# A two-layer hybrid block on one core: the instruction order from the tile scheduler's timeline simulation

## The chip, the cores and the metric

The program runs on one core of a Trainium2 chip. The time is the device time of one execution in microseconds (us). A core has a matrix engine (PE), a vector engine (DVE), a scalar engine (ACT), GpSimd (POOL) and a queue that issues transfers (SP). Each engine takes its instructions strictly in the order of its own program, and semaphores make it wait for the others. The change is about that order and about nothing else.

## What is computed

Two layers of a block for 256 tokens of `x` and 256 of a context, width 1024, all in float32. Each layer normalises, mixes tokens by three branches (a spatial gate, a differential attention, a gated delta net in both directions), merges them, and ends in a gated convolution network of width 2816. Cut to what matters:

```python
for l in range(DEPTH):                                   # DEPTH = 2
    mod_x, mod_c = silu(c) @ w_mod[l] + b_mod[l], silu(c_ctx) @ w_mod[l] + b_mod[l]
    h_x = modulate(rms_norm(x, norm1_g[l]), sh1_x, sc1_x)     # and h_c for the context
    (u, sv, bq, bk, bv, dq, dk, dv, dz, beta, a, gate) = split_in(h @ w_in[l])
    ya = gelu(u) * (w_s @ rms_norm(gelu(sv)) + b_s)           # spatial gating
    p = softmax(q k^T); yb = rms_norm((p[:, 0] - lam * p[:, 1]) @ v)   # differential attention
    # gated delta net, chunks of 64 tokens, both directions
    u, w = triangular_solve(I + A, v * beta), triangular_solve(I + A, k * beta * exp(G))
    def step(state, blk):
        v_new = u_c - w_c @ state
        o_c = qd_c @ state + intra_c @ v_new
        state = state * g_tot + k_tail^T @ v_new
    yc = rms_norm(o) * silu(z)
    y = (sig(g0) * (ya @ w_a) + sig(g1) * (yb @ w_b) + sig(g2) * (yc @ w_c)) @ w_o
    x = x + gt1 * y
    x = x + gt2 * (silu(conv(h @ w_up)_gate) * conv(h @ w_up)_val) @ w_down
```

The context is carried through layer 0 only.

## The kernel before

All large products run on PE in three passes of a reduced-precision type: each operand is split into a high and a low part (`wh`, `wl` for weights, `hh`, `hl` for activations), and `wh*hh`, `wl*hh` and `wh*hl` are added up in one PSUM bank. A weight block arrives by SP in `wr` (3 buffers); ACT makes `wh` from it and DVE `wl` (4 buffers each). PSUM has eight banks in four groups: `p` two, `g` three, `a` two and `b` one. Nearly every instruction is recorded at a helper's line (L240 matmul, L237 activation, L219 tensor-tensor, L234 scalar-tensor-tensor, L231 tensor-scalar), so the tile names tell them apart.

The names that the steps below use, in the order of a layer (`mixer`, L629):

- The modulation products `pmod`, `pmc` and `modv` (head of the program), and, for later use, rows of `wmt` with DVE products `mj` (L483), issued ahead of their need.
- `norm_halves` (L539): `pss` and `pb` on PE, `xn` on DVE, then `hh` on ACT and `hl` on DVE, for eight blocks of the width.
- `pu`, `ptm`, `pj`, `pg`: projections by PE, long runs of matmuls that need nothing but weights and `hh`, `hl`. They fill PE while a chain elsewhere goes on. `pj` writes a buffer that the scan's `U` occupies until the scan is done, so `pj` can't start before it.
- `gdn_solve` (L1210): a chain of 31 steps on DVE (`sT`, `sL`) ends in `sLC`; then PE does 128 small products `pZ`, ACT copies them to `sZ` and lays out `U`, PE does 128 products `pU2`, ACT copies those into `U`, DVE scales `U`.
- `gdn_intra` (L1088): `pkv`, `pgram` on PE, `vtok` on ACT, `inT` on DVE.
- `gdn_scan` (L1181) calls `gdn_step` (L1285) eight times. A step can't begin before the state `gS` of the one before it is there, and alternates between PE and DVE:

```python
pk = kT @ S                     # PE, pkS
rhs = pk * neG + vtok           # DVE, four instructions
V = U @ rhs                     # PE, pV
vn = V * tail (and V * r2)      # DVE
pq = qT @ S; po = inT @ vn      # PE, pq and pgo, in the steps that give an output
S = S * gts + ktok^T @ vn       # PE, pS (two products), then DVE, gS
```

- `attn_core` (L871): scores `psc` (PE), maximum `mx` (DVE), exponentials (ACT), `pr` (DVE), transposes `paT` (PE, L907) and their copy `aT` (ACT), `po` (PE), a norm on DVE, transposes `poT` (PE, L922).
- `gdn_out` (L1357): four groups of transposes `pgT` (L1362) in layer 0, two in layer 1, all in the one bank of group `b`; four DVE instructions empty it each time.
- `branch` (L689): `pg` and `pbr`, the latter from the branch's result (`ych`, `ycl` for the delta net).

What sets the order: the kernel's text is one long program, and the scheduler that wraps it (`tile.TileContext`) sorts all instructions of all engines by a simulated machine, which takes from the instructions that are ready. `gdn_keys`, `gdn_solve`, `gdn_intra`, `gdn_scan` and `gdn_out` stand in `tc.high_priority(offset=AHEAD)` blocks, which lets the scheduler put them ahead of work that the text names earlier. Which model of the machine it simulates decides how many matmuls of `pu`, `ptm` or `pg` it puts between two links of a chain.

## Time and profile before

| | |
|---|---|
| median of three runs (lowest, highest) | 1647.09 us (1644.26, 1651.51) |
| the profiled execution | 1642.39 us, its span 1640.6 us |
| PE busy | 1583.4 us, 97% of the span |
| DVE busy | 1207.0 us, 74% |
| ACT busy | 767.9 us, 47% |
| mean granted clock of PE | 0.985 of full speed |

The span runs from the first instruction to the last; 1.8 us of the execution lie outside it. "Busy" is the union of an engine's instructions, so on PE it counts a matmul from its start to its modelled end.

### The profile page before, as it was taken

How to read it: one execution, taken by the hardware profiler on the slowest of the kernel's cores; microseconds unless marked ns; L12 is line 12 of the kernel's file. 1: busy time of each engine (PE TensorE's matmuls, PEld its weight loads, DVE VectorE, ACT ScalarE, POOL GpSimd, SP SyncE). 2: the span in 40 equal slices, each digit the busy share in tenths (PEclk: the TensorE clock that was granted, in tenths of full speed). 3: DMA queues.
4: the chain of work that ended last, by engine and by line, in shares of the span. 5: the costliest groups of instructions: out<-in, count | busy, mean ns of one | idle time of the engine just before them, and what ended most of it. 6: DMA issues, size and time to landing. Idle time of an engine off the chain costs nothing.

```text
span 1640.6 us, 27599 instructions
## 1 busy us (share of the span) xinstructions
PE 1583.4 (97%) x10664; PEld 1346.9 (82%) x10664; DVE 1207.0 (74%) x2831; ACT 767.9 (47%) x1455; POOL 6.6 (0%) x16
## 2 busy tenths in 40 slices
PE   5999999999999998999999999999999999989999
PEld 3777977876788887888888887888878799989998
DVE  5649977788764457999778876659777776788685
ACT  3654461156532333544234443654723754556563
POOL 0000000000000000000000000000000000000000
PEclk9999989999999998999999999999999999989999
DMA  8313321142343433454566565221222246545655
GB/s 340 132 60 110 107 66 53 65 125 69 100 145 94 150 93 101 128 171 160 166 203 201 191 195 182 78 92 53 70 64 83 86 144 223 186 132 180 191 181 154
DMA packets 65283, 218.22 MB, mean 133 GB/s; under 512 B 7552, under 2 KB 13696, under 8 KB 63232
## 3 DMA queue, kind: packets, MB, share of 16 engines
q1 hardware_dynamic: 63280, 208.70, 39.9%
q10 hardware_dynamic: 1872, 7.77, 1.3%
q8 instruction: 83, 1.36, 0.3%
q14 instruction: 48, 0.39, 0.1%
HBM read 213.29 MB, written 3.15 MB: 132 GB/s over the span
## 4 chain that ended last, share of the span: by engine, by line
PE 83%; DVE 7%; ACT 4%; DMA 2%; issue 2%; ACTq 0%; DVEq 0%
PE pup L240 21%; PE pg L240 12%; PE pdn L240 10%; PE pqkv L240 7%; PE pbr L240 6%; PE ptm L240 4%; PE pwo L240 4%; PE pu L240 2%; PE psc L240 2%; PE pj L240 2%; PE pS L240 2%; ACT U L237 1%; DMA wmt<-in_wmt_dram 1%; PE pkS L240 1%; PE po L240 1%
## 5 line engine op out<-in xcount | busy, mean ns | idle before, releaser
L237 ACT ACTIVATE wh<-wr 128x512 fp32r<-128x512 f32 (+1 forms) x594 | 366.7, 622 | 432.1 <-PE pdn L240 91.1
L219 DVE TENSOR_TENSOR wl<-wr,wh 128x512 fp32r<-128x512 f32 (+1 forms) x592 | 399.4, 680 | 156.8 <-ACT wh L237 154.1
L240 PE MATMUL pup<-hh,wh 128*128 128x256 f32 (+1 forms) x720 | 242.3, 337 | 2.2 <-ACT hh L237 2.1
L240 PE MATMUL pup<-hh,wl 128*128 128x256 f32 (+1 forms) x720 | 241.4, 336 | 0.0
L240 PE MATMUL pup<-hl,wh 128*128 128x256 f32 (+1 forms) x720 | 240.3, 335 | 0.0
L240 PEld LDWEIGHTS pup<-hh,wh 128*128 128x128 f32 x720 | 139.1, 193 | 16.8 <-ACT hh L237 2.9
L240 PEld LDWEIGHTS pup<-hh,wl 128*128 128x128 f32 x720 | 139.1, 193 | 13.0
L240 PEld LDWEIGHTS pup<-hl,wh 128*128 128x128 f32 x720 | 138.4, 193 | 13.1
L240 PE MATMUL pg<-hh,wh 128*128 128x512 f32 (+1 forms) x384 | 131.0, 341 | 0.1
L240 PE MATMUL pg<-hh,wl 128*128 128x512 f32 (+1 forms) x384 | 130.4, 339 | 0.2 <-DVE wl L219 0.2
L240 PE MATMUL pg<-hl,wh 128*128 128x512 f32 (+1 forms) x384 | 130.2, 339 | 0.0
L240 PE MATMUL ptm<-wh,hl 128*128 128x256 f32 x448 | 130.2, 291 | 0.0
L240 PE MATMUL ptm<-wl,hh 128*128 128x256 f32 x448 | 129.6, 289 | 0.3 <-DVE wl L219 0.3
L240 PE MATMUL ptm<-wh,hh 128*128 128x256 f32 x448 | 129.4, 289 | 0.0
L234 DVE SCALAR_TENSOR_TENSOR fcv<-pup,par,fcv 128x510 f32<-128x510 f32 (+1 forms) x176 | 107.3, 612 | 26.2 <-ACT fcv L237 26.1
L240 PE MATMUL pdn<-fh,wh 128*128 128x256 f32 (+1 forms) x366 | 121.0, 330 | 0.7 <-ACT fh L237 0.7
L240 PE MATMUL pdn<-fl,wh 128*128 128x256 f32 (+1 forms) x366 | 120.6, 330 | 0.7 <-DVE fl L219 0.7
L240 PE MATMUL pdn<-fh,wl 128*128 128x256 f32 (+1 forms) x366 | 120.7, 330 | 0.0
L483 DVE SCALAR_TENSOR_TENSOR wmt<-wmt,scb 128x1024 f32<-128x1024 f32 x80 | 97.7, 1221 | 23.1 <-DMA wmt<-in_wmt_dram 22.6
L240 PEld LDWEIGHTS ptm<-wh,hh 128*128 128x128 f32 x448 | 86.6, 193 | 2.7 <-issue 2.0
L240 PEld LDWEIGHTS ptm<-wl,hh 128*128 128x128 f32 x448 | 86.6, 193 | 2.5 <-issue 1.7
L240 PEld LDWEIGHTS ptm<-wh,hl 128*128 128x128 f32 x448 | 86.7, 194 | 2.1 <-issue 1.7
(332 smaller groups left out, 3223.1 us busy)
## 6 DMA issues: line engine op xcount, KB each, us to landing
wmt<-in_wmt_dram SPq DMA_DIRECT2D x80, 512.0 KB, 3.6
wr<-in_wup_dram SPq DMA_DIRECT2D x80, 512.0 KB, 3.9
wr<-in_wfm_dram SPq DMA_DIRECT2D x78, 512.0 KB, 3.5
wr<-in_wtm_dram SPq DMA_DIRECT2D x32, 512.0 KB, 3.6
wr<-in_wdn_dram SPq DMA_DIRECT2D x32, 512.0 KB, 3.9
wr<-in_wbr_dram SPq DMA_DIRECT2D x24, 512.0 KB, 3.6
wm<-in_wmod_dram SPq DMA_DIRECT2D x8, 1024.0 KB, 11.0
wr<-in_wo_dram SPq DMA_DIRECT2D x16, 512.0 KB, 3.5
```

Source lines behind the costliest of these rows:

```text
L219: self.nc.vector.tensor_tensor(out=out, in0=a, in1=b, op=op)
L234: self.nc.vector.scalar_tensor_tensor(out=out, in0=a, scalar=s, in1=b, op0=op0, op1=op1)
L237: self.nc.scalar.activation(out, a, f, bias=bias, scale=scale, **k)
L240: self.nc.tensor.matmul(out, lhsT, rhs, start=start, stop=stop, **k)
L483: nc.vector.scalar_tensor_tensor(out=o, in0=w, scalar=1.0, in1=sb[:, v], op0=ALU.mult, op1=ALU.mult, accum_out=m4[:, n % 4, v:v + 1])
```

## The change

One argument is added where the scheduler is created. With it the scheduler simulates the machine by its timeline simulation in place of its default model. No instruction, tile, buffer or transfer is added or taken away by the kernel's text.

```diff
--- before.py
+++ after.py
@@ -1452,7 +1452,7 @@
     out = nc.dram_tensor("out_0_dram", (128, 8, SEQ), F32, kind="ExternalOutput").ap()
-    with tile.TileContext(nc) as tc:
+    with tile.TileContext(nc, schedule_with_timeline_sim=True) as tc:
         body(tc, aps, out)
```

Both programs have the same 9364 matmuls on PE and 2703 instructions on DVE; ACT has the same activations and 25 loads of its function table where there were 29. What differs is the order: nearly all of PE's rows and most of DVE's have moved. Three places follow, all on PE; in a row the tile written stands left of the arrow, with the number that the kernel's text gives it, and `x8` counts equal matmuls in a row.

Place 1, PE between the solve and the scan of layer 0, the last rows ahead of the scan's first `pV`. Before:

```order
L240 MATMUL pgram_2424<-qT_616,kT_188 64x64 x8
L240 MATMUL pu_3056<-hl_125,wh_3063 128x512
L1096 MATMUL pkv_2434<-cst0_77,vT_617 128x128 x4
L240 MATMUL pu_3056<-hh_124,wh_3063 128x512
L240 MATMUL pgram_2440<-qT_616,kT_188 64x64 x8
L240 MATMUL pu_3056<-hh_124,wl_3064 128x512
L1096 MATMUL pkv_2450<-cst0_77,vT_617 128x128 x4
L240 MATMUL pu_3056<-hl_125,wh_3063 128x512
L240 MATMUL pgram_2456<-qT_616,kT_188 64x64 x8
L240 MATMUL pu_3056<-hh_124,wh_3063 128x512
L240 MATMUL pu_3056<-hh_124,wl_3064 128x512
L240 MATMUL pV_2467<-vtok_2401,U_1312 64x128 x8
```

Now:

```order
L1096 MATMUL pkv_2402<-cst0_77,vT_617 128x128 x4
L240 MATMUL psc_3807<-akT_1414,qhT_1413 128x256
L240 MATMUL psc_3810<-akT_1414,qhT_1413 128x256
L240 MATMUL pgram_2408<-qT_616,kT_188 64x64 x8
L1096 MATMUL pkv_2418<-cst0_77,vT_617 128x128 x4
L240 MATMUL pgram_2424<-qT_616,kT_188 64x64 x8
L1096 MATMUL pkv_2434<-cst0_77,vT_617 128x128 x4
L240 MATMUL pgram_2440<-qT_616,kT_188 64x64 x8
L1096 MATMUL pkv_2450<-cst0_77,vT_617 128x128 x4
L240 MATMUL pgram_2456<-qT_616,kT_188 64x64 x8
L240 MATMUL pV_2467<-vtok_2401,U_1312 64x128 x8
L240 MATMUL pu_3139<-hh_124,wh_3142 128x512
```

The `pu` matmuls that stood between `pkv`, `pgram` and `pV` are gone from there; the whole of `pu_3056` and `pu_3097` and four `psc` now stand ahead of `pZ`, and two further `psc` stand among the rows shown.

Place 2, PE in the second half of the scan of layer 0 (`pkS_2806` opens a step). Before:

```order
L240 MATMUL pgo_2776<-vn_2764,inT_1043 64x128 x8
L240 MATMUL pS_2788<-vn_2764,ktok_1041 128x128 x4
L240 MATMUL pS_2797<-vn_2764,ktok_1041 128x128 x4
L240 MATMUL pkS_2806<-gS_2466,kT_188 64x128
L240 MATMUL pu_3181<-hh_124,wh_3188 128x512
L240 MATMUL pu_3181<-hh_124,wl_3189 128x512
L240 MATMUL pu_3181<-hl_125,wh_3188 128x512
L240 MATMUL pu_3181<-hh_124,wh_3188 128x512
L240 MATMUL pu_3181<-hh_124,wl_3189 128x512
L240 MATMUL pu_3181<-hl_125,wh_3188 128x512
L240 MATMUL pu_3181<-hh_124,wh_3188 128x512
L240 MATMUL pu_3181<-hh_124,wl_3189 128x512
```

Now:

```order
L240 MATMUL pV_2755<-rhs_2750,U_1312 64x128 x2
L240 MATMUL pq_2767<-gS_2466,qT_616 64x128 x8
L240 MATMUL pV_2755<-rhs_2750,U_1312 64x128 x6
L240 MATMUL pgo_2776<-vn_2764,inT_1043 64x128 x8
L240 MATMUL pS_2788<-vn_2764,ktok_1041 128x128 x4
L240 MATMUL pS_2797<-vn_2764,ktok_1041 128x128 x4
L240 MATMUL pkS_2806<-gS_2466,kT_188 64x128 x8
L240 MATMUL pV_2820<-rhs_2815,U_1312 64x128 x2
L240 MATMUL pq_2832<-gS_2466,qT_616 64x128 x8
L240 MATMUL pV_2820<-rhs_2815,U_1312 64x128 x6
L240 MATMUL pgo_2841<-vn_2829,inT_1043 64x128 x8
L240 MATMUL pS_2853<-vn_2829,ktok_1041 128x128 x4
```

Before, 5 to 13 matmuls of `pu` or `ptm` stood between the links of a step; now the last four steps follow each other with nothing between. (A float32 matmul of these rows is two in the trace, so `x8` here is `x16` there.)

Place 3, PE at the end of the attention and in `gdn_out` of layer 0. Before:

```order
L240 MATMUL pbr_4613<-yal_4304,wh_4605 128x512
L240 MATMUL pbr_4613<-yah_4303,wh_4605 128x512
L922 MATMUL poT_4297<-cst0_77,on_4158 128x128 x4
L240 MATMUL pbr_4613<-yah_4303,wl_4606 128x512
L240 MATMUL pbr_4613<-yal_4304,wh_4605 128x512
L240 MATMUL pbr_4613<-yah_4303,wh_4605 128x512
L240 MATMUL pbr_4613<-yah_4303,wl_4606 128x512
L1362 MATMUL pgT_4807<-cst0_77,go_2488 128x128 x4
L240 MATMUL pbr_4613<-yal_4304,wh_4605 128x512
```

Now:

```order
L907 MATMUL paT_4238<-cst0_77,pr_4221 128x128 x4
L240 MATMUL po_4245<-vB_1415,aT_4243 128x128 x4
L907 MATMUL paT_4269<-cst0_77,pr_4252 128x128 x4
L240 MATMUL po_4276<-vB_1415,aT_4274 128x128 x4
L922 MATMUL poT_4297<-cst0_77,on_4158 128x128 x4
L1362 MATMUL pgT_4807<-cst0_77,go_2488 128x128 x4
L1362 MATMUL pgT_4816<-cst0_77,go_2546 128x128 x4
L1362 MATMUL pgT_4825<-cst0_77,go_2785 128x128 x4
L1362 MATMUL pgT_4834<-cst0_77,go_2850 128x128 x4
L240 MATMUL pbr_4905<-ych_4843,wh_4897 128x512
L240 MATMUL pbr_4905<-ych_4843,wl_4898 128x512
L240 MATMUL pg_4921<-hh_124,wh_4924 128x512
```

Before, 9 or 10 matmuls of `pg` and `pbr` stood between two `pgT`, and over a hundred ahead of `pbr_4905`; now the last links of the attention, the four `pgT` and the first `pbr_4905` that needs their result follow each other directly.

## Rows read from the trace of the kernel before

**Rows 1.** The page: busy time of each engine, and the chain that ended last.

```profile
PE 1583.4 (97%) x10664; PEld 1346.9 (82%) x10664; DVE 1207.0 (74%) x2831; ACT 767.9 (47%) x1455; POOL 6.6 (0%) x16
...
PE 83%; DVE 7%; ACT 4%; DMA 2%; issue 2%; ACTq 0%; DVEq 0%
```

**Rows 2.** Windows: stretch, its length, busy us (instructions) by engine, clock, DMA share, GB/s.

```profile
core 0: us, PE busy (x) PEld busy (x) DVE busy (x) ACT busy (x) POOL busy (x), PEclk, DMA share, GB/s
0.00:40.00 40.00, 21.71 (x191) 14.04 (x192) 22.57 (x56) 14.56 (x25) 1.32 (x6) 1.00 0.87 339
160.00:200.00 40.00, 39.47 (x327) 38.68 (x326) 39.90 (x134) 16.24 (x28) 0.00 (x0) 1.00 0.40 124
400.00:440.00 40.00, 40.00 (x191) 26.69 (x190) 29.23 (x84) 23.63 (x67) 0.00 (x0) 1.00 0.23 67
640.00:680.00 40.00, 35.02 (x209) 31.64 (x208) 36.08 (x90) 19.67 (x37) 0.00 (x0) 0.87 0.33 106
```

**Rows 3.** Windows, from first pZ to first pV of each layer, all instructions.

```profile
207.10:230.90 23.80, 20.55 (x371) 17.37 (x370) 14.35 (x40) 21.11 (x34) 2.07 (x4) 0.78 0.15 46
1163.80:1184.30 20.50, 17.97 (x347) 16.45 (x346) 13.03 (x37) 20.17 (x32) 2.07 (x4) 0.83 0.18 54
```

**Rows 4.** The same windows, PE alone: tile pu in layer 0, ptm in layer 1.

```profile
core 0: us, PE busy (x), PEclk, DMA share, GB/s
207.10:230.90 23.80, 6.93 (x20) 0.78 0.15 46
...
1163.80:1184.30 20.50, 7.39 (x35) 0.83 0.18 54
```

**Rows 5.** Timeline of PE: start, length, instruction, count, [idle before it <-releaser].

```profile
222.72 0.69 PE L240 MATMUL pgram<-qT,kT 128*64 128x64 f32 x16 [3.25 <-ACT U L237]
...
230.88 1.09 PE L240 MATMUL pV<-vtok,U 64*64 64x128 f32 x16
```

**Rows 6.** Timeline of PE in gdn_scan: step of layer 0, then one of layer 1.

```profile
247.01 0.66 PE L240 MATMUL pkS<-gS,kT 128*64 128x128 f32 x8
...
253.65 1.09 PE L240 MATMUL pgo<-vn,inT 64*64 64x128 f32 x16
...
254.67 1.71 PE L240 MATMUL pS<-vn,ktok 64*128 64x128 f32 x16
...
256.31 0.43 PE L240 MATMUL pkS<-gS,kT 128*64 128x128 f32 x2
...
1197.05 0.44 PE L240 MATMUL pkS<-gS,kT 128*64 128x128 f32 x4
...
1204.52 0.43 PE L240 MATMUL pkS<-gS,kT 128*64 128x128 f32 x2
```

**Rows 7.** Timeline of DVE within that step of layer 0.

```profile
248.74 1.13 DVE L234 SCALAR_TENSOR_TENSOR rhs<-pkS,g_neG,vtok 128x128 f32<-128x128 f32 x4 [0.40 <-PE pkS L240]
...
251.62 0.69 DVE L219 TENSOR_TENSOR vn<-pV,g_tail 128x512 f32<-128x512 f32 x1 [1.16 <-PE pV L240]
...
255.86 0.35 DVE L234 SCALAR_TENSOR_TENSOR gS<-gS,g_gts,pS 128x128 f32<-128x128 f32 x1 [0.38 <-PE pS L240]
```

**Rows 8.** Timeline of PE: end of the attention and gdn_out, layer 0; gdn_out, layer 1.

```profile
427.22 1.55 PE L240 MATMUL psc<-akT,qhT 64*128 64x512 f32 x4
...
435.27 0.66 PE L907 MATMUL paT<-cst,pr 128*128 128x128 f32 x4
...
436.70 1.08 PE L240 MATMUL po<-vB,aT 128*128 128x128 f32 x8
...
441.09 0.66 PE L922 MATMUL poT<-cst,on 128*128 128x128 f32 x4
...
1324.65 0.66 PE L1362 MATMUL pgT<-cst,go 128*128 128x128 f32 x4
...
1326.81 0.60 PE L1362 MATMUL pgT<-cst,go 128*128 128x128 f32 x4
```

**Rows 9.** Windows at the lower clock: after the idle of Rows 5, and in norm_halves.

```profile
223.41:226.81 3.40, 3.40 (x24) 2.56 (x24) 2.53 (x5) 2.85 (x7) 0.00 (x0) 0.50 0.02 5
646.66:656.86 10.20, 6.84 (x29) 6.46 (x30) 9.45 (x35) 3.40 (x8) 0.00 (x0) 0.50 0.35 105
```

**Rows 10.** Timeline of DVE in norm_halves of layer 0.

```profile
651.23 1.08 DVE L219 TENSOR_TENSOR xn<-xn,pb 128x256 f32<-128x256 f32 x3 [0.65 <-PE pb L240]
```

## Prediction

> **What bounds the kernel now.** I read the page first. PE is busy for 1583.4 of 1640.6 us, and the chain that ended last is PE for 83% [rows 1]. The instructions and their operands stay as they are, so PE's 1583 us stay too, and the change can only add to or take from the 57 us in which PE stands still. Then the windows: PE is full where `pg` and `pbr` accompany the attention, and short by 18.3 us in the first 40 and by 5.0 us around `norm_halves` of layer 0 [rows 2]. Of the 18.3 the most is the load of the first operands, which no order removes. So the most that can be won is small, and what can be lost depends on how well the new order covers the three chains in which PE and another engine wait for each other: solve to scan, the scan's steps, the attention's end with `gdn_out`. There I read the timelines of PE and DVE.
>
> Before, these chains are covered. The solve's DVE chain fills its stretch (39.90 of 40 us on DVE) and PE has 39.47 us of other work there [rows 2]. A scan step runs from `pkS` to `pkS` in 9.30 us in layer 0 and 7.47 us in layer 1, without an idle mark on PE [rows 6]. Inside the step it is DVE that waits for PE, three times, 1.94 us together [rows 7]. That PE waits is the exception: 3.25 us ahead of `pgram`, for ACT's copies out of the bank that it needs [rows 5].
>
> **The change part by part.** All durations are of the profiled execution (1642.39 us; 1.8 us outside the span), and the sum is made against it. It lies 4.7 us below the median of the three runs.
>
> *Ahead of the solve's end.* The new order gives DVE 56 more instructions ahead of `sLC` in layer 0 and 60 in layer 1, an estimate of 21 and 19 us, and PE 19 and 21 us of `pu`, `ptm` and `psc`. Both engines were full there, so both ends move together: +0 to +2.4 us in layer 0 (the difference), taken +1, and nothing in layer 1. This alone is harmless. What matters is that this PE work is then gone from behind.
>
> *From `pZ` to the first `pV`.* This took 23.8 us in layer 0 with PE busy for 20.55 [rows 3]. Of the 20.55, 6.93 are `pu` [rows 4] and about 3 are 8 `ptm` and 4 `pqkT`; the first place of the order shows them gone and two `psc` (about 0.5) in their stead. So 11 us of PE work are left to cover a chain that runs PE, ACT (the copies into `U`), DVE, PE. If the chain keeps 23.8 us, PE idles 12.8; if it shrinks to the 20.5 us that layer 1 shows [rows 3], 9.5. It idled 3.25 before [rows 5], so the loss is 6.3 to 9.5 us; I take 7, near the lower end, since `pgram` no longer queues behind `pu`. In layer 1, 17.97 busy less 7.39 of `ptm` [rows 3, 4] and some 1.6 of `pqkT`, plus the `psc`, leave 9.4. A chain of 18.3 to 20.5 us gives 8.9 to 11.1 idle, against 2.5 before: +6.4 to +8.6, taken +7.5. Two steps: **+14.5** (12 to 18).
>
> *The scan.* Its second place in the order: the last four steps of layer 0 and the last five of layer 1 have nothing between their links, because `pu` and `ptm` are used up and `pj` waits for `U`'s buffer. A step with output then holds 6.5 us of PE work (16 matmuls each of `pkS`, `pV` and `pq`, 1.25 us apiece, `pgo` 1.09, `pS` 1.71 [rows 6]; 6.5 to 7.0 by summing the trace's starts over the new order), one without 4.3. The bare chain was never seen, since PE was always busy. It is no longer than 9.30 us; without output, where it lacks `pq` and `pgo`, 7.47 [rows 6]. Taking off the time in which DVE waited for PE behind foreign matmuls, about 1 us, I take 8.5 to 9.3 and 7.5. So a step with output loses 2 to 2.8 us, one without 3.2. Layer 0: three full steps, a wait of 1.4 ahead of the first of them and 1.5 in the last: **+9.5** (8 to 11.5). Layer 1: one step at 3.2, three at 2.4, and the last: **+11** (8.5 to 13).
>
> *Attention's end and `gdn_out`.* Its third place: 14 us of chain now stand back to back. The `psc` pair to its last `paT` took 8.05 us, of which some 2 were DVE's other work, against 3.2 us of PE work there now: 2 to 4 us lost. `paT` to `po` 1.43 less the 0.60 that `paT` itself takes: 0.8. `po` to `poT` 4.39 [rows 8] less 1.08: 3.3. `poT` to `pgT`, behind `yb` in the same bank: 0.8. Each further `pgT` waits until DVE has emptied the bank: 2.16 us apart at layer 1 [rows 8], of which 0.6 is work, so 1.6 three times, 4.7. Then DVE's and ACT's split ahead of `pbr_4905`, about 2. Layer 0: **+14.5** (12.4 to 16.8). In layer 1 two `pgT` and the `po` wait are left, `pg` covers the rest: **+4.7** (3.5 to 6). Of the PSUM bank the Trainium skill has a rule ("Perfetto Trace Analysis", Matmuls): independent matmul groups should rotate through different banks so that emptying one overlaps the next. Four `pgT` in one bank are its counter-example. By the rule's remedy, a second bank, the 4.7 us would be close to zero; this kernel has one, and the 2.16 us between its `pgT` agree with the rule.
>
> *`norm_halves`.* DVE now makes all eight `xn` (0.36 us each [rows 10]) and in layer 0 an `mj` ahead of the first `hl`; before, three. Five `xn` and the `mj` are 3.0 us, and in layer 1 1.8, part of it beside PE's products with `hh`: **+3.7** (1 to 5).
>
> *Head and rest.* `pmod` and `pmc` stand earlier, so `modv` and the second `hh` come earlier; of the idle time that isn't loading I expect **-4** back (-5 to -2). For that SP now issues 4.1 MB of modulation rows and constants ahead of two weight blocks `wr`; at the head's 339 GB/s [rows 2] they delay these by 12 us, to about 39 us, and PE comes to them at about 47, so nothing waits; were PE 10 us ahead, the gain would be gone. Small waits in the network: **-1** (-2 to 0). ACT's four table loads less cost nothing or gain nothing: ACT is busy for 47% [rows 1].
>
> *The clock.* After 3.25 us without work PE ran 3.40 us at a granted 0.50, its lower level of 1.2 GHz; around `norm_halves`, where short waits repeat, it was 10.2 us [rows 9]. At the lower level matmuls take about twice as long, so such a stretch costs 1.7 us, or up to 3.4 of PE's 6.84 busy us. Two solves, one attention's end and a scan's tail at that price: **+8** (3, if only the solves; 38, if all nine bare steps run at the lower level, where about 4 us of each are PE's links). I take the low end's side because a bare step still keeps PE at work for two thirds of its time. The Trainium skill ("TensorE: Matmul & The Clock Gate", Part 1) tells of two levels, which the rows show, and advises to count less than 1% of a span for the warming up; by that the term would be at most 16 us, while the rows alone allow 38.
>
> **Sum:** 1 + 14.5 + 9.5 + 11 + 14.5 + 4.7 + 3.7 - 4 - 1 + 8 = 61.9, so 1642.4 + 61.9 = **1704 us**. All low ends give +41 (1683), all high ends +109 (1751). Against the median of before that is +3.5%; 0.5%, 8 us, is about what a measurement of this kernel can tell from no change.
>
> **The rivals.**
>
> *A: the bare chains are short, and it gets faster.* The bare step was never seen. DVE has less beside the scan in the new order (5.8 to 6.4 us a step, where it had 7.1 to 9.6), and it waited for PE inside the step [rows 7]. If a bare step needs no more than its 6.5 us of PE work, and the attention's end is as quick, the scan's and the end's terms vanish. Solve to scan then decides: with a chain of 14 us in each layer nothing is lost and 3.25 + 2.5 are won. With the head's 4 and 1 the time is 1642.4 - 11 = 1631. Against it: DVE's four `rhs`, two `vn` and `gS` are links of the chain and no PE work runs beside them; 1.13 + 1.4 + 0.35 [rows 7] on top of PE's own links make more than 6.5.
>
> *B: no change.* Half of A: the scan stays covered by what is left of `ptm`, and only solve to scan is exposed, with the head's gain against it: 14.5 and 3.7 for `norm_halves`, less 5 for the head and 5 for a quicker chain, is +8 at most, or 1642 to 1650. Against it: the bare rows of the order.
>
> *C: the clock falls through.* In nine bare steps and the attention's end PE works in short pieces between waits, as around `norm_halves` [rows 9]. With 38 in the place of 8 the time is 1734. The same page of the Trainium skill (HAM oscillation) describes such a kernel, in which each burst after a wait starts at the lower level. For it: the 10.2 us; against it: those waits had less PE work between them.
>
> *D: the flag does nothing.* The order shows nearly all of PE's rows moved, so I give this no chance.
>
> **How the numbers follow.** Slower as in the sum, 0.70 (1655 to 1720); C, 0.13 (1720 to 1740 and beyond); B, 0.08; A, 0.09. The range of 1650 to 1735 leaves out A, most of B and the end of C, together 0.2. Faster by over 0.5%: 0.09; within: 0.08; slower: 0.83.
>
> **What would show it.** In the changed profile PE should lack 25 to 30 us more in the two scans with `pkS` 8 to 9 us apart in the last four steps and idle marks that name DVE (`rhs`, `vn`, `gS`); about 10 us idle between `pU2` and the first `pV`, named after ACT's `U`; four `pgT` some 2.2 us apart with idle between them; and a first `pqkv` with `hh` of the second half earlier than before. It would be wrong if the bare steps are 7 us, or if PE's clock stays down through the scan, or if a stretch that I took as equal, above all the network (half of the span), has new waits of its own: 0.1 us in each of its 88 projections would be 9 us.

## The result: 1768 us, slower by 7.5%, and where the time went

The changed kernel takes 1767.99 us (median of 4 runs, 1762.89 to 1782.56) beside 1645.99 us of the kernel before on the same chip: a ratio of 1.0746 with an interval of 1.071 to 1.0781. I had forecast 1704 us with a range up to 1735. The direction was right, the size about half of what came. The profiled execution took 1771.99 us, 129.6 more than that of before.

From the page of the changed kernel: busy time by engine, the granted clock in 40 slices (9 is full), and the chain that ended last.

```profile
PE 1615.6 (91%) x10664; PEld 1377.8 (78%) x10664; DVE 1213.3 (69%) x2831; ACT 756.7 (43%) x1451; POOL 6.6 (0%) x16
...
PEclk9989879779988999999999999999878899999999
...
PE 68%; DMA 12%; DVE 11%; issue 4%; ACT 4%; SPq 0%; DVEq 0%; ACTq 0%
```

Beside [rows 1], PE's busy time has grown by 32.2 us, with the same 10664 instructions, and the span by 129.6. So PE stands still for 154.6 us where it stood for 57.2: **97.4 us are waits, 32.2 are longer busy time.** PE's share of the chain fell from 83% to 68%; DMA, which had 2%, has 12%, a share that nothing in my sum stands for. The slices of the clock hold four values below 8, where the solve and the scan's last steps of layer 0 and `pZ` to `pV` of layer 1 lie.

The next table cuts both spans at PE's first instruction of a tile. The idle time is the length less PE's busy time in the windows of the two traces. Work also moves across such borders, so a row's length by itself says less than its idle time.

| stretch, from one tile to the next | before, us (PE idle) | after, us (PE idle) | more | more idle |
|---|---|---|---|---|
| head, to the second `psq` of layer 0 | 107.4 (22.3) | 121.5 (27.2) | 14.1 | 4.9 |
| solve, `pZ` to `pV`, scan of layer 0, to `pj` | 225.7 (6.6) | 262.9 (36.3) | 37.2 | 29.7 |
| `pj` to `pbr_4905`: attention and `gdn_out` | 142.2 (0.3) | 154.5 (12.8) | 12.3 | 12.5 |
| to `pup`, with `norm_halves` | 176.9 (5.0) | 179.6 (5.5) | 2.7 | 0.5 |
| network of layer 0, to `pss_9313` | 364.6 (0.7) | 387.6 (17.6) | 23.0 | 16.9 |
| to the second `psq` of layer 1 | 76.4 (6.0) | 82.9 (6.7) | 6.5 | 0.7 |
| solve to `gdn_out` of layer 1, to `pwo_14071` | 319.6 (7.4) | 355.2 (40.2) | 35.6 | 32.8 |
| the rest | 227.8 (8.9) | 226.0 (8.3) | -1.8 | -0.6 |

Five of the stretches as windows of the changed kernel (length, busy us of PE, PEld, DVE, ACT, POOL, granted clock, DMA share, GB/s): `pZ` to `pV` of layer 0, the end of its scan with what follows up to `pj`, `pj` to `pbr_4905`, the network, `pZ` to `pV` of layer 1.

```profile
244.80:267.90 23.10, 15.79 (x340) 13.11 (x340) 8.13 (x18) 17.81 (x29) 2.07 (x4) 0.51 0.01 1
327.60:384.40 56.80, 40.55 (x337) 33.15 (x337) 38.15 (x132) 2.08 (x4) 1.12 (x2) 0.67 0.07 19
384.40:538.90 154.50, 141.73 (x652) 105.08 (x652) 113.67 (x300) 74.15 (x186) 0.00 (x0) 0.94 0.32 103
718.50:1106.10 387.60, 370.00 (x1678) 302.03 (x1679) 293.57 (x533) 142.62 (x250) 0.00 (x0) 1.00 0.52 163
1282.50:1304.70 22.20, 15.17 (x311) 11.64 (x310) 6.75 (x13) 18.20 (x30) 2.07 (x4) 0.50 0.01 2
```

**From `pZ` to `pV`** the stretch has lost its cover as forecast: PE's busy time falls from 20.55 to 15.79 us and from 17.97 to 15.17 [rows 3]. But it is also at the clock's lower level from end to end, 0.51 and 0.50, where before it was at 0.78 and 0.83. The idle time is 7.3 and 7.0 us, against 3.25 and 2.5. Most of it stands where it stood before [rows 5], behind ACT's copies into `U`; in layer 0:

```profile
260.39 1.12 PE L240 MATMUL pgram<-qT,kT 128*64 128x64 f32 x16 [6.54 <-ACT U L237]
```

**Ahead of the solve's end**, where I had +1 and 0, PE lost 9.4 us in layer 0 and 6.4 in layer 1. Its timeline (start, length, instruction, [idle before it <-releaser]) shows where, two of the waits:

```profile
209.75 1.11 PE L850 MATMUL pqkT<-cst,axc 128*128 128x128 f32 x4 [2.53 <-DVE axc L219]
...
212.34 0.58 PE L240 MATMUL ptm<-wh,hh 128*128 128x256 f32 x1 [1.48 <-ACT axq L237]
```

The instructions pulled forward there, `ptm`, `pqkT` and `psc`, have chains of their own through `axq`, `axc` and `pr` on ACT and DVE, and DVE was busy for 110 of 123 us there. The longest waits by releaser are 2.74 us for DVE's `wl` in layer 0 and 5.71 us for ACT's `axq` in layer 1. I had counted their length on each engine and not that they wait for one another.

**The scan's last steps** in the same view, first of layer 0, then of layer 1:

```profile
337.80 2.54 PE L240 MATMUL pkS<-gS,kT 128*64 128x128 f32 x16
...
340.94 0.69 PE L240 MATMUL pV<-rhs,U 64*64 64x128 f32 x4 [0.60 <-DVE rhs L234]
...
346.49 1.97 PE L240 MATMUL pgo<-vn,inT 64*64 64x128 f32 x16 [1.48 <-DVE vn L219]
...
351.94 1.98 PE L240 MATMUL pkS<-gS,kT 128*64 128x128 f32 x16 [0.46 <-DVE gS L234]
...
364.84 1.43 PE L240 MATMUL pkS<-gS,kT 128*64 128x128 f32 x8
...
1358.06 1.21 PE L240 MATMUL pkS<-gS,kT 128*64 128x128 f32 x14 [0.58 <-DVE gS L234]
...
1367.11 1.21 PE L240 MATMUL pkS<-gS,kT 128*64 128x128 f32 x16 [0.92 <-DVE gS L234]
...
1376.41 1.21 PE L240 MATMUL pkS<-gS,kT 128*64 128x128 f32 x14 [0.60 <-DVE gS L234]
```

A step is the distance from one `pkS` with 14 or 16 matmuls to the next: in layer 1 9.05 and 9.30 us, at full clock, inside the 8.5 to 9.3 that I had estimated, with idle marks after DVE's `gS`, `rhs` and `vn`. (Two `pkS` can start a microsecond ahead of the 14; from the first `pkS` of a step the two steps are 10.1 and 8.3 us.) In layer 0 it is 14.1 and 12.9 us: `pkS` takes 2.54 and 1.98 us where it takes 1.21 at full clock, `pS` some 3.1 instead of 1.7. The same chain runs at the lower level here.

Behind the scan comes a wait that my sum doesn't have:

```profile
379.92 3.75 PE L240 MATMUL pmix<-sguwb,gv 128*128 128x128 f32 x16 [6.01 <-DMA sguwb<-in_sguw_dram]
```

```profile
375.87 1.11 DVE L234 SCALAR_TENSOR_TENSOR gS<-gS,g_gts,pS 128x128 f32<-128x128 f32 x4
```

```profile
377.02 0.34 ACTq L734 DMA_DIRECT2D sguwb<-in_sguw_dram  x1
```

The spatial gate's product `pmix` needs `sguwb`, whose transfer goes into the one buffer that the scan's state `gS` occupies (both tiles have the tag `gS`, L732 and L1183). So it follows the scan in either order: ACT issues it right behind the last `gS` on DVE, which ends at 376.98 us here and at 316.03 us before (issues at 377.02 and 316.06). Before, PE had 111 matmuls of `ptm` to do until `pmix` at 329 us; now nothing is left to cover the transfer. It is one more link of the bare chain. In layer 1 the same product waits 3.85 us for DVE's `gv`.

**The attention's end and `gdn_out`** of layer 0, to be read beside [rows 8]:

```profile
527.07 1.12 PE L922 MATMUL poT<-cst,on 128*128 128x128 f32 x4 [3.30 <-DVE on L219]
...
528.96 1.11 PE L1362 MATMUL pgT<-cst,go 128*128 128x128 f32 x4 [0.78 <-ACT yb L237]
...
531.48 1.09 PE L1362 MATMUL pgT<-cst,go 128*128 128x128 f32 x4 [1.40 <-DVE z L234]
...
534.31 1.09 PE L1362 MATMUL pgT<-cst,go 128*128 128x128 f32 x4 [1.75 <-DVE z L234]
...
536.71 1.09 PE L1362 MATMUL pgT<-cst,go 128*128 128x128 f32 x4 [1.31 <-DVE z L234]
...
538.91 0.80 PE L240 MATMUL pbr<-ych,wh 128*128 128x512 f32 x1 [1.11 <-ACT ych L237]
```

The 3.30 us ahead of `poT` are what I had written, the `pgT` follow each other 2.40 to 2.83 us apart, and PE stands still for 1.31 to 1.75 us between them, after DVE's `z`, which empties their one bank. That is the counter-example of the Trainium skill's rule on rotating banks ("Perfetto Trace Analysis", Matmuls), and these rows agree with it.

**The network of layer 0**, which I had put at -1, lost 23.0 us. Two groups of the page (busy us, mean ns | idle time before them, releaser):

```profile
L240 PE MATMUL pup<-hh,wl 128*128 128x256 f32 (+1 forms) x720 | 241.9, 337 | 10.7 <-DVE wl L219 10.7
...
L483 DVE SCALAR_TENSOR_TENSOR wmt<-wmt,scb 128x1024 f32<-128x1024 f32 x80 | 97.6, 1220 | 46.4 <-DMA wmt<-in_wmt_dram 46.3
```

The same two groups before:

```profile
L240 PE MATMUL pup<-hh,wl 128*128 128x256 f32 (+1 forms) x720 | 241.4, 336 | 0.0
...
L483 DVE SCALAR_TENSOR_TENSOR wmt<-wmt,scb 128x1024 f32<-128x1024 f32 x80 | 97.7, 1221 | 23.1 <-DMA wmt<-in_wmt_dram 22.6
```

One place of the loss, DVE first (start, length), then the issue on SP, then PE:

```profile
860.94 1.23 DVE L483 SCALAR_TENSOR_TENSOR mj<-wmt,scb 128x1024 bf16<-128x1024 f32 x1 [3.75 <-DMA wmt<-in_wmt_dram]
...
862.09 0.69 DVE L219 TENSOR_TENSOR wl<-wr,wh 128x512 fp32r<-128x512 f32 x1
```

```profile
856.67 0.33 SPq L478 DMA_DIRECT2D wmt<-in_wmt_dram  x1
```

```profile
859.81 0.39 PE L240 MATMUL pdn<-fh,wh 128*128 128x512 f32 x1
862.83 0.50 PE L240 MATMUL pdn<-fh,wl 128*128 128x512 f32 x1 [2.63 <-DVE wl L219]
```

`wmt` has one buffer. SP issues the next transfer of it at 856.67, it lands after about 4 us, and DVE's next instruction in its order is the `mj` that reads it. DVE stands still for 3.75 us, and the `wl` behind it in the same queue, whose `wr` and `wh` have long been there, comes only at 862.09. PE waits 2.63 us for that `wl`. The trace has 21 gaps of PE in this stretch where before there was 1, together 17.5 us, of which 15.5 end with DVE's `wl`. PE's busy time grows by the other 6 us of the 23 although the clock is 1.00; by my reading this is overlap between neighbouring matmuls that is lost at each gap. In net0_old_dve below, where 3 gaps are left, the busy time is back at 363.4 us (363.8 before).

**The head** lost too: the first `psq`, in the norm of the keys, waits longer than the 2.63 us of before.

```profile
92.39 0.80 PE L240 MATMUL psq<-cst,sse 128*128 128x4 f32 x3 [6.09 <-ACT sse L237]
```

### The profile page after: what moved, and what is told of

It reads as the page before. It is cut to its first block, busy times and chain, and to the rows that moved or that the text cites. A ratio compares the mean times of both kernels' runs of the same rounds, so it can differ in the third digit from the quotient of the medians.

```text
span 1770.2 us, 27621 instructions
## 1 busy us (share of the span) xinstructions
PE 1615.6 (91%) x10664; PEld 1377.8 (78%) x10664; DVE 1213.3 (69%) x2831; ACT 756.7 (43%) x1451; POOL 6.6 (0%) x16
## 4 chain that ended last, share of the span: by engine, by line
PE 68%; DMA 12%; DVE 11%; issue 4%; ACT 4%; SPq 0%; DVEq 0%; ACTq 0%
PE pup L240 13%; PE pg L240 11%; DMA wmt<-in_wmt_dram 10%; PE pdn L240 7%; PE ptm L240 7%; PE pqkv L240 6%; PE pbr L240 6%; PE pwo L240 4%; PE pu L240 2%; PE pj L240 2%; DVE wmt L483 2%; PE psc L240 2%; ACT U L237 1%; DVE wl L219 1%; PE pV L240 1%
## 5 line engine op out<-in xcount | busy, mean ns | idle before, releaser
L237 ACT ACTIVATE wh<-wr 128x512 fp32r<-128x512 f32 (+1 forms) x594 | 363.4, 621 | 418.5 <-PE pdn L240 73.7
L240 PE MATMUL pup<-hl,wh 128*128 128x256 f32 (+1 forms) x720 | 236.2, 334 | 1.4 <-DVE hl L234 1.3
L240 PEld LDWEIGHTS pup<-hh,wh 128*128 128x128 f32 x720 | 138.0, 192 | 16.9 <-ACT hh L237 2.7
L240 PE MATMUL ptm<-wh,hl 128*128 128x256 f32 x448 | 129.6, 290 | 0.0
L483 DVE SCALAR_TENSOR_TENSOR wmt<-wmt,scb 128x1024 f32<-128x1024 f32 x80 | 97.6, 1220 | 46.4 <-DMA wmt<-in_wmt_dram 46.3
```

What stands on the lines that cost most here:

```text
L237: self.nc.scalar.activation(out, a, f, bias=bias, scale=scale, **k)
L240: self.nc.tensor.matmul(out, lhsT, rhs, start=start, stop=stop, **k)
L483: nc.vector.scalar_tensor_tensor(out=o, in0=w, scalar=1.0, in1=sb[:, v], op0=ALU.mult, op1=ALU.mult, accum_out=m4[:, n % 4, v:v + 1])
```

## Experiments

My theory after the two traces had three causes: chains that lie bare (waits of PE for DVE and ACT at solve, scan and attention's end), the clock in them, and in the network DVE's order around `wmt`. The first rival was that DVE's new order makes all of it; the second was that the clock falls wherever a chain is bare, so that waits and clock are one cause.

All experiments but out_warm are the same program with the same instructions. What differs is the order. A function behind `body` adds order-only dependencies between the listed instructions of an engine, so that they are issued in the listed order, and the scheduler places everything else by its own model:

```diff
         body(tc, aps, out)
+        pin(tc, nc)
...
+def pin(tc, nc):
...
+            if last is not None:
+                tc.add_manual_dep(have[name], last, mybir.DependencyInfo(
+                    mybir.DependencyClass.NoSync, mybir.DependencyReason.DATA), reason="pin")
+            last = name
```

The list is a table of numbers; I tell in words what it holds. Where it says "with the flag", the line of the change is in the kernel too:

```diff
-    with tile.TileContext(nc) as tc:
+    with tile.TileContext(nc, schedule_with_timeline_sim=True) as tc:
```

Each median stands beside one of the kernel before that was measured with it on the same chip.

### Which part of the program: one part at a time in the new order

Without the flag, all engines' instructions of one part are held in the order of the changed kernel: the head (head_new), the mixer of layer 0 (mix0_new), its network (net0_new), the mixer of layer 1 (mix1_new).

> The default model, but the head (up to the keys' norm of layer 0, instructions 76 to 899) is held in the order of the changed kernel; the rest as before. Theory L (the 122 us are a sum of local losses, of which the network, layer 0's mixer and layer 1's mixer have shown 15, 52 and 32): the head loses 10 to 20 us, the wait of psq for sse 6 us in the place of 2.6; time 1656 to 1666. Rival J (what is left over arises only where the parts come together): within 4 us of 1646.

> The default model, but layer 0's mixer (from the first norm's end to the last pwo) is held in the order of the changed kernel on every engine; the rest as before. Theory L (the 122 us are a sum of local losses): the mixer's stages lose here what they lost there, 37 us from the solve to the end of the scan and 12 us to the first pbr of the delta net, less up to 10 us if PE's clock stays up in the scan; time 1646 + 39 to 50, 1685 to 1696. Rival H (the mixer's loss is inherited from the late head): under 1670.

> The default model, but layer 0's network is held in the order of the changed kernel on every engine; everything else is as before. Theory N: the network's idle time is 15 to 20 us here too, and the time is 1646 + 15 to 20, about 1663. Rival M: the mixer is as before, so nothing is late, and the time is within 5 us of 1646.

> The same for layer 1's mixer. Theory L: 36 us from the keys' norm to pwo and up to 8 us at the first norm; 1646 + 33 to 44, 1679 to 1690. Rival H (inherited from what comes before): under 1665.

| part in the new order | median, us | before, us | ratio (interval) | more |
|---|---|---|---|---|
| head | 1653.08 | 1646.81 | 1.0038 (1.0023 to 1.0053) | 6.3 |
| mixer of layer 0 | 1698.21 | 1645.74 | 1.0316 (1.0299 to 1.0334) | 52.5 |
| network of layer 0 | 1662.85 | 1647.41 | 1.0092 (1.0069 to 1.0114) | 15.4 |
| mixer of layer 1 | 1678.09 | 1645.74 | 1.0193 (1.0176 to 1.021) | 32.4 |

The four together are 106.6 of the 122 us. The head loses less than the 10 to 20 us that I had expected, layer 0's mixer 2.5 us more than my upper end; the signs of my head and network terms are refuted by runs that hold nothing else. The other 15 us appear only when the parts stand together, and the traces show no single place for them. Cut at the borders of the table above, the changed kernel is longer than the run with that part alone by 6.5 us in the head, 2.2 us from the solve of layer 0 to `pj`, 5.7 us in the network and 7.3 us in the mixer of layer 1, and shorter by 1.9 us from `pj` to `pbr_4905`: some 20 us, between single executions. The clock has a part in it. The four bare steps of layer 0 take 46.4 us in the changed kernel and 37.8 in mix0_new, where all of PE's 320 instructions stand in the same order. Windows of them, first the changed kernel, then mix0_new:

```profile
327.60:374.00 46.40, 36.76 (x320) 29.62 (x320) 29.54 (x94) 0.49 (x2) 1.12 (x2) 0.67 0.04 13
```

```profile
322.20:360.00 37.80, 25.68 (x320) 19.84 (x320) 29.40 (x94) 0.47 (x2) 1.12 (x2) 1.00 0.04 15
```

The clock is 0.67 in the one and 1.00 in the other, 8.6 us; elsewhere from the solve to `pj` mix0_new is 6.4 us longer. In the mixer of layer 1 the changed kernel is at the lower level for 68.3 us, mix1_new for 47.8, with PE in the same order; the stretch is 35.6 us longer than before in the one and 28.3 in the other. What decides which of the two levels such a stretch meets, I could not settle: the changed kernel itself spreads from 1763 to 1783 us between runs with a mean clock from 0.952 to 0.936.

### The network: DVE's queue or PE's order

With the flag, the network of layer 0 is held in the order of before: on all engines (net0_old), or on DVE alone (net0_old_dve).

> The flag is on, but the instructions of layer 0's network (norm_halves, pup, pdn, and what stands there of wmt and mj) are held in the order of before on every engine; the rest is ordered as in the changed kernel. Theory N (the network's own order costs: DVE takes an mj or wmt instruction at its head before the transfer of wmt has landed, and wl waits behind it): PE's idle time between the first pup and the last pdn of layer 0 falls from about 18 us to about 1, and the time by 15 to 20 us, from 1768 to about 1750. Rival M (the network waits because the mixer before it has left the modulation rows late): the idle time stays, and the time is within 5 us of 1768.

> The flag is on; of layer 0's network only DVE's instructions are held in the order of before, PE, ACT and SP are free. Theory N (it is the place of mj and wmt in DVE's queue that costs): as with all engines held, 1745 within 5 us, and PE's waits for wl there are gone. Rival P (it is PE's own order in the network): 1760 to 1770, waits for wl as in the changed kernel.

net0_old: 1745.02 us, 1.0601 (1.0564 to 1.0638), 23 us less than the changed kernel. net0_old_dve: 1742.32 us, 1.062 (1.0583 to 1.0656), the same. So the loss is gone with DVE's old order, whether the other engines are held or not. PE is free in net0_old_dve, and its order there is neither that of before nor the new one. But in pe_new, further down, PE has the new order and DVE is not held, and the network is 15 us shorter than in the changed kernel. It is DVE's order that costs here. The two groups of the page, first net0_new (PE and DVE both new), then net0_old_dve (DVE as before):

```profile
L240 PE MATMUL pup<-hh,wl 128*128 128x256 f32 (+1 forms) x720 | 241.6, 336 | 6.4 <-DVE wl L219 6.4
...
L483 DVE SCALAR_TENSOR_TENSOR wmt<-wmt,scb 128x1024 f32<-128x1024 f32 x80 | 97.7, 1222 | 36.9 <-DMA wmt<-in_wmt_dram 36.7
```

```profile
L240 PE MATMUL pup<-hh,wl 128*128 128x256 f32 (+1 forms) x720 | 240.2, 335 | 0.0
...
L483 DVE SCALAR_TENSOR_TENSOR wmt<-wmt,scb 128x1024 f32<-128x1024 f32 x80 | 97.6, 1220 | 36.6 <-DMA wmt<-in_wmt_dram 36.2
```

In both DVE waits for `wmt` for 36 us. With the new order that costs PE 6.4 us in this group; with DVE's old order it costs nothing, because what stands behind the waiting instruction isn't what PE needs next. How long a queue waits says little; what is queued behind it says it. In the traces the network is 19.9 us (net0_old) and 22.9 us (net0_old_dve) shorter than the 387.6 us of the changed kernel, and in net0_new 17.4 us longer than before. The 23 us of the medians need not all be its own: in net0_old the scan of layer 0, which was not touched, ran at full clock,

```profile
326.40:364.20 37.80, 25.68 (x320) 19.82 (x320) 29.41 (x94) 0.47 (x2) 1.12 (x2) 1.00 0.05 15
```

which is the 8.6 us of above again. The network's own part lies between the 15.4 us of net0_new and 23 us.

### Whose order: PE's or DVE's, over the whole program

Without the flag, all of PE (pe_new) or all of DVE (dve_new) is held in the changed kernel's order.

> The default model orders DVE, ACT and SP, but PE is held in its order of the changed kernel from the first matmul to the last. Theory P (in the mixers it is PE's order that costs, by chains that have no matmuls between their links): the scan, gdn_out and the stretch from pZ to pV lose what they lose in the changed kernel, 50 to 60 us with the lower clock on top; time 1710 to 1750. Rival D (it is what DVE does ahead of those links): PE's order alone costs under 20 us; time below 1666.

> The default model orders PE, ACT and SP, but DVE is held in its order of the changed kernel. Theory P: only the network's wait for wmt (15 to 20 us) and some of the solve (up to 15 us) are lost; time 1660 to 1685. Rival D: 1700 or more.

pe_new took 1753.49 us, 1.0636 (1.0598 to 1.0674): with PE held, 106 of the 122 us are there, and what is lacking is by its size the network, which in its trace is 15 us shorter than in the changed kernel. In the mixers this doesn't separate PE from DVE, though. DVE was free and followed PE: from the second `psq` of layer 0 to `pZ` it does 332 instructions, where it did 273 before and 333 in the changed kernel. dve_new took 1824.33 us, 1.108 (1.105 to 1.111), worse than the change itself and far from my expectation. It doesn't bear out the rival that DVE's order makes all of it, though: the scheduler, given DVE's order, also moved PE's `pu` and `ptm` ahead of the chains, so the run has both effects in a third order (no `pu` or `ptm` is left from `pZ` to `pV` of either layer). It separates nothing. Between engines that wait for each other, holding one doesn't leave the other as it was, and the free engine's resulting order has to be read before such a run is relied on. What refutes that rival for the bare chains are the next runs, in which DVE keeps all but a few dozen of its rows.

### Bare chains without the rest

Without the flag and in the order of before, PE's filling matmuls (`pu`, `ptm`, `pj`, `pg`, `pbr`) between the first and the last instruction of a chain are moved behind it. scan_bare: the last four steps of the scan in layer 0 and the last five in layer 1. out_bare: from the last `psc` pair to the last `pgT` in layer 0. out_pz_bare: the same and `pZ` to `pV` in layer 1.

> Order of before, with one thing changed: in the last four steps of the scan of layer 0 and the last five of layer 1 all matmuls of pu and ptm (89 and 86) stand behind the last pS on PE; the default model orders the other engines. Theory B (bare steps cost by themselves): a step with output takes 8.5 to 9.3 us if PE's clock stays up, against 6.5 us of PE work, so about 11 us are lost in each layer and the time is 1647 + 22 = 1669; where the clock falls to its lower level a step takes 13 to 14 us, as in layer 0 of the changed kernel, and the loss is up to 28 us a layer, time up to 1703. Rival S (the scan's loss in the changed kernel comes from what other engines do beside it, transfers and copies that the new order puts there): PE's bare order costs under 8 us in all; time below 1655.

> Order of before, only the 72 matmuls of pg and pbr at the end of layer 0's attention put behind the last pgT. It is the first half of the kernel with two bare places, where that stretch was 19.6 us longer; so 1646 + 17 to 20, 1663 to 1666, with PE's clock at its lower level from the last paT to the first pbr.

> Order of before, with two things changed: at the end of layer 0's attention the 72 matmuls of pg and pbr between the last psc pair and the last pgT stand behind that pgT, and in layer 1 the 34 matmuls of ptm between pZ and the scan's first pV stand behind that pV; the default model orders the other engines. Theory B: 10 to 13 us of PE idle time at layer 0's attention (pgT to pgT 2.2 to 2.5 us) and 5 to 9 us at layer 1's pZ, some 3 us for the clock; time 1647 + 18 to 25, about 1668. Rival S: other engines' order is what costs; time below 1655.

scan_bare: 1658.31 us, 1.0082 (1.0068 to 1.0097), +13.7, between the 1669 of theory B and the 1655 of rival S. The bare steps take 8.3 to 10.2 us, the idle time grows by 7.5 and 6.4 us, and the clock stays up. Windows of the two scans:

```profile
271.10:307.00 35.90, 28.11 (x322) 20.51 (x321) 27.72 (x92) 0.81 (x3) 1.12 (x2) 1.00 0.06 16
1225.00:1258.00 33.00, 26.64 (x320) 20.41 (x320) 23.33 (x61) 0.90 (x2) 0.00 (x0) 1.00 0.07 19
```

Both are less than the 9.5 and 11 of my prediction and lie under its ranges; in layer 1 the steps are 7.7 to 9.4 us. Above all it refutes the second rival for the scan: bare chains with PE at work for 78% and 81% of the time, and in mix0_new for 68%, keep the full clock. (For the other two places it isn't refuted: each trace here in which `pZ` to `pV` or the attention's end lies bare has the lower level there.) That the chain of layer 0 lost it in the changed kernel has no cause that the trace shows: PE had waited 1.4 us in the 59.7 ahead of it, 1.5 in net0_old, where the clock stayed up, and 1.4 in pe_new, where it fell.

out_bare: 1667.21 us, 1.0124 (1.0106 to 1.0141), +21.5, just above my 17 to 20. The idle time grows by 13.2 us, near the 14.5 of the sum; what comes on top shows in the window, 27.3 us at the lower level.

```profile
432.40:459.70 27.30, 15.74 (x53) 12.08 (x54) 12.20 (x40) 6.79 (x17) 0.00 (x0) 0.50 0.06 20
```

out_pz_bare: 1673.3 us, 1.0172 (1.0157 to 1.0187), +28.7, a little above the 18 to 25 that I had expected. Its profile is 19.6 us longer from `pj` to `pbr_4905`, by the attention's end, and 5.9 us longer from `pZ` to the first `pkS` of layer 1 (30.5 instead of 24.6); another 4.4 us lie just ahead of that `pZ`, where the list leaves PE as before but 10.2 us are at the lower level.

### Can the clock be kept up, or the order be bettered

out_warm is out_bare with 34 useless 128x512 matmuls in the waits, 11 ahead of `poT` and 5 or 6 ahead of each `pgT`. They write a bank that nobody reads.

```diff
+        warm = self.bank("a", "warm") if l == 0 else None
         for t, ot in outs:
+            for j in range(0 if warm is None else 16 if t == outs[0][0] else 6):
+                self.mm(warm, self.hh[:, 0, 0:128], self.hh[:, j % 8, :])
             p = self.bank("b", "pgT")
```

> The same with 34 further matmuls of no use (128x512, into a PSUM bank that nobody reads) ahead of poT and of each pgT, 0.23 us each, so that PE works where it waited. Theory C (part of a bare stretch's loss is the lower clock, not the wait): the clock stays up, the transposes and the matmuls behind them take half as long, and the kernel is 3 to 6 us faster than the same without them although it does 7.9 us more of PE work. Rival W (only the waits count): the same time, or up to 5 us slower where the added matmuls stand in the way.

1665.88 us, 1.0108 (1.0088 to 1.0127): 1.3 us below out_bare, which the two intervals don't tell apart; the 3 to 6 us of theory C don't show in the program's time. In the two traces the stretch from `pj` to `pbr_4905` is 3.7 us shorter with the added matmuls (159.7 and 163.4 us). The clock did rise. Windows of out_warm, then the end of `gdn_out` on PE in out_bare and in out_warm:

```profile
437.70:447.90 10.20, 7.15 (x25) 5.68 (x24) 3.99 (x17) 3.10 (x11) 0.00 (x0) 0.50 0.19 53
447.90:457.20 9.30, 8.77 (x47) 6.67 (x47) 5.69 (x16) 2.88 (x5) 0.00 (x0) 1.00 0.00 0
```

```profile
451.24 1.09 PE L1362 MATMUL pgT<-cst,go 128*128 128x128 f32 x4 [1.31 <-DVE z L234]
...
453.64 1.09 PE L1362 MATMUL pgT<-cst,go 128*128 128x128 f32 x4 [1.31 <-DVE z L234]
```

```profile
454.65 0.63 PE L1365 MATMUL pgT<-cst,go 128*128 128x128 f32 x4 [0.22 <-DVE z L234]
...
456.59 0.63 PE L1365 MATMUL pgT<-cst,go 128*128 128x128 f32 x4
```

From 447.9 on PE is at 1.00 and a `pgT` takes 0.63 in place of 1.09 us, but the next one still comes 1.9 to 2.2 us behind it, where it was 2.4, since it waits for DVE's `z`. PE's clock is worth little where another engine is the link.

pz_mix5 and pz_mix8 go the other way: one filling matmul behind every fifth, or every eighth, of the small products `pZ` and `pU2`, so that this stretch isn't bare at all. norm_net1 takes the wait of DVE for `wmt` out of `norm_halves` of layer 0, by putting those products behind the last `hl`, and gives PE the new order in the network of layer 1.

> An attempt at a better order by what the runs show of the clock: as before, but one matmul of ptm or pu stands behind every fifth of the small pZ and pU2 products (25 in each layer), taken from those that follow them; the scan's last steps have that many less. If it is the small products that let the clock fall there, it stays up, 3.4 us a layer are won, and some of the 3.25 and 2.5 us that PE waited behind; against that up to two bare steps a layer at 2 us: time 1636 to 1646. If the clock falls all the same, or ACT's copies come later by the matmuls put between, 1646 to 1655.

> The same with one behind every eighth (16 in each layer): half of that gain and of that loss; 1640 to 1648.

> An attempt at a better order by the default model: in norm_halves of layer 0 the mj and wmt pairs (2.4 us) that DVE does between the links of the inverse root and among hl stand behind the last hl, and in layer 1's network PE is held in the order of the changed kernel, where that stretch took 226.0 us against 227.8. If both gains come, 2.3 and 1.8 us, the time is about 1643; if the transfers of wmt that are put back by 10 us hold up the network's modulation, 1650 or more.

All three lose, the first two by more than any of my cases allowed. pz_mix5: 1673.95 us, 1.0174 (1.0156 to 1.0191). pz_mix8: 1670.94 us, 1.0148 (1.0128 to 1.0168). The window of pz_mix5, and the first of ACT's copies:

```profile
217.60:241.50 23.90, 23.90 (x207) 14.56 (x206) 6.86 (x28) 15.81 (x24) 2.07 (x4) 0.50 0.20 66
```

```profile
216.75 1.20 ACT L237 ACTIVATE sZ<-pZ 32x512 f32<-32x512 f32 x2 [3.31 <-PE pZ L240]
```

PE is busy for 23.90 of 23.90 us, and at the lower level for all of it. With fill between them the small products end later, so ACT's copies wait (3.31 us, and 3.52 us in the next pair), and `pZ` to `pV` takes 40.3 us instead of 23.8. norm_net1: 1651.5 us, 1.004 (1.0027 to 1.0053): `norm_halves` won 2 us, and the network behind it lost 10 in the trace, 6.6 of them at one place. DVE's row, then PE's:

```profile
672.26 1.22 DVE L483 SCALAR_TENSOR_TENSOR mj<-wmt,scb 128x1024 bf16<-128x1024 f32 x1 [3.56 <-DMA wmt<-in_wmt_dram]
...
675.42 0.79 PE L240 MATMUL pup<-hh,wl 128*128 128x512 f32 x1 [6.61 <-DVE wl L219]
```

The `mj` that was put back waits 3.56 us for `wmt`, with the `wl` that PE needs behind it: the mechanism of the network once more, made by hand. The 1.8 us that I had hoped for in layer 1's network aren't the order's: head_new, which leaves that stretch as before, is 1.8 us shorter there too. No order that I tried is faster than the kernel before.

## Why the prediction was right in direction and wrong in size

The steps that failed are three terms set near or below nothing (ahead of the solve's end, the network, the head), a missing link behind the scan, and the size of the clock's term. The mechanism of the bare chains was right.

- **Right: what bounds the kernel, and the bare chains.** PE was full, its fill is what covers the chains, and with the fill gone they wait. Of the scan's terms, 9.5 and 11 us, PE stands still for 9.6 us of the 46.4 in layer 0, and in layer 1 for 10.3 of the 39.3 us from 1344.7 us on, with 2.4 ahead of it. That the first fits is in part luck. I had priced steps at full clock; there the same four steps stand still for 12.1 of 37.8 us (mix0_new), above my range, and one of them takes 11.0 us from `pkS` to `pkS`, where I had called 9.30 an upper bound after reading one step. The attention's end, 14.5, measures 12.5 idle; in layer 1 4.7 became 3.0 (1.20 us ahead of `poT`, 0.78 and 1.38 ahead of the two `pgT`, less 0.32 before).
- **Too large: `pZ` to `pV`**, 14.5 against 8.6 of added idle time. The chain wasn't short, 23.1 and 22.2 us, the second above my 18.3 to 20.5; but at the lower clock the work that is left keeps PE busy for 15.8 and 15.2 us, where I had counted 11 and 9.4. Also `norm_halves`, 3.7 against 1.2 in both layers.
- **Wrong: ahead of the solve's end, +1 and nothing.** It was +9.4 and +6.4. The step added up what each engine does there and took full engines for covered chains. The work moved forward has waits of its own, as the releasers in the trace name them; no run isolates them.
- **Wrong: the network, -1.** It was +23 (15.4 alone, by net0_new). I had named new waits in the network as what would make the prediction wrong, with 9 us as an example, and put none into the sum or the range, although DVE's order there was to be had. The place to look was the 80 products with `wmt`, which has one buffer and for which DVE already waited 22.6 us before: behind which of them the new order puts a `wl` that PE needs soon.
- **Wrong: the head, -4.** Alone it costs 6.3 us, in the changed kernel 4.9 us of idle time and more in clock. Two waits for ACT carry it: 6.09 us in place of 2.63 ahead of `psq`, and 2.22 us for `wh` at 41.83 us, where PE had no wait before.
- **Missing:** the transfer of `sguwb` behind the scan, 6.0 us, and `gv`, 3.85 us, in layer 1. I had seen that `pj` waits for the buffer of the scan's `U`, and not that this transfer waits for the buffer of its state.
- **Too small: the clock, 8 in a range of 3 to 38.** Busy time grew by 32.2 us; 6 of that is the network's, at full clock, so by an estimate about 26 stand for the clock. PE was at the lower level for 207.6 us, of which it was busy for 152.0; before it was 50.5 and 39.6. That is 11.7% of the span at the lower level, and 1.5% of it by the estimate of its cost. The Trainium skill's figure of under 1% of a typical span for warming up ("TensorE: Matmul & The Clock Gate", Part 1), at most 18 us here, is below that estimate. My argument for the low end was that a bare step keeps PE at work for two thirds of the time; for the scan alone it was right (scan_bare at 1.00), in the whole it was not. The case of the clock falling through, C, was the nearer one: the estimate of 26 is closer to its 38 than to my 8. At 1734 it lacked the network and the solves.

The sum's errors are some 14.8 ahead of the solves, 24 in the network (23.0 and the 1 that I had taken off), 8.9 in the head, 9.9 behind the scans and 18 of clock, less 12.1 of terms that were too large: 63.5. With them the sum is 125.4 beside 129.6 measured; the rest I can't assign. A range whose upper end holds only the terms that were thought of is too narrow when one flag moves all of the program.

## What to carry to other kernels

A new instruction order is priced by its queues: for every instruction that can wait (above all one that reads a single-buffered transfer) look at what stands behind it on its engine and who needs that. Engines that are full add up to no covered chain; work that is pulled forward brings its own waits. A stretch that the new order lays bare may meet either level of PE's clock: both prices belong into the range, and raising the clock is worth little where another engine is the link.

## What the runs showed of the hardware that was not expected

- A PE that the profile shows as busy without a gap isn't thereby at full clock: in pz_mix5 it was busy for all of 23.90 us, with small 32x32 products and a 128x512 matmul behind every fifth of them, at a granted 0.50.
- The same 320 instructions of PE in the same order took 46.4 us at 0.67 and 37.8 us at 1.00, in kernels that differ elsewhere; a bare scan by itself stayed at 1.00.
- A wait of PE between matmuls of the network costs more than its length: 16.9 us more idle time came with 6 us more of busy time at full clock, by an estimate 0.3 us for each of the 20 additional gaps.
